# Hi and lo parts of late weights made in the up projection of an encoder layer, and loaded again where they are used

## The chip, the cores and the metric

The kernel runs on one core of one Trainium2 chip. The metric is the device time of one execution in microseconds, the median of several runs.

## The reference

One encoder layer in fp32, with 1024 tokens, width 1024 and a hidden width of 4096. The change touches the last two steps:

```
x = x + (gate_a * y_a + gate_b * y_b) @ w_out            # both attention branches
h = rmsnorm(x, norm_mlp_g)
x = x + square(relu(h @ w_ff1)) @ w_ff2                  # up, then down
gate_p = sigmoid(rmsnorm(x, norm_ple_g) @ w_ple_gate)    # 1024 x 1024
x = x + gate_p * (p @ w_ple)                             # p: 1024 x 256
return rmsnorm(x, final_norm_g)
```

## The kernel before

Every fp32 product is made of three matmuls. An operand is split into a hi part (a copy rounded to float32r, on ScalarE, L235) and a lo part (source minus hi, on VectorE unless another engine is named, L236), and `mm3` (L239) multiplies hi by hi, hi by lo and lo by hi. A matmul is written as 128x512: 128 partitions by 512 columns. Loads and stores go through SyncE's queue (`load`, L232).

Stages in order: input mixing with both attention branches, output mixing with x1 (the residual, also stored to DRAM), the up projection, the down projection, and the per-layer embedding with the final norm. All arrays live in regions of SBUF that open and close: a region that opens over a closed one waits until the old one's readers are done.

**Up (`up`, L1090).** 16 pairs, each 256 columns of `w_ff1`, and each a 2x2 block product by Winograd's scheme, 7 products of 12 matmuls, 84 in all. Per pair SyncE loads w1 into one of two slots (`raw2`), GpSimd makes four sums of its quarters, ScalarE and VectorE split them into the ring `rc` (6 slots of 2048). `relu2` squares the result on ScalarE and stores u (chunks of 128 rows, 32 in all) to DRAM. At the start the normalised input, in four quarters (`hf`), is combined and split into the regions `ha`, `hb` and `hc`.

**Down (`down`, L1150).** 8 blocks of 4 chunks of u and the matching rows of w2. Blocks 0 to 6 are done by Winograd: GpSimd makes the eight sums s and t (L1177 to L1184), both operands are split into `rc`, and each product is added in PSUM order into one of seven accumulators `facc` (VectorE, L1206). Block 7, the plain one, is done directly: its 4 rows of w2 are split (lo on GpSimd), then for each of 8 row tiles u is split, 24 matmuls run, the accumulators are gathered into x1 (44 sums of 128x512, on GpSimd for one column half and VectorE for the other, L1227) and the PSUM result is added (L1252).

**Embedding (`ple`, L1268).** 8 rows of the gate and 2 of the embedding weight are loaded and split (`ple_weights`, `w_rows`). Per row tile, `prepare` loads p, transposes it (L1294), norms and transposes x (L275) and splits both; `finish` runs 48 gate and 12 embedding matmuls, the sigmoid, the product, the final norm and the store.

The order on each engine is set by a scheduler from the program's dependences, unless a stretch is put under `manual_schedule`, which keeps one engine's instructions in the order of the code.

Of the kernel before, what the change touches and what calls it, by code (L numbers as in the profile page):

```python
# [17 lines left out]
P = 128  # L18
S = 1024
# [22 lines left out]
N_GW = 7  # L42

# [182 lines left out]
class Layer:  # L226
# [79 lines left out]
    def run(self):  # L306
# [23 lines left out]
        self.wg, self.rg = [], []  # L330
        self.up()
        self.down()
        self.ple()
# [667 lines left out]
    def mix_outputs(self):  # L1001
# [37 lines left out]
        self.hf = [self.rf[i].take(2048) for i in (0, 1, 1, 0)]  # L1039
# [50 lines left out]
    def up(self):  # L1090
# [15 lines left out]

        def relu2(j, i, u):
            nc.scalar.activation(u, u, AF.Relu)
            nc.scalar.activation(u, u, AF.Square)
            self.load(self.dr["u"][2 * j + i], u)  # L1110
# [35 lines left out]
        wi.run([job(j) for j in range(2, n_pair)], cur)  # L1146
        for region in left[::-1]:
            region.close()

    def down(self):  # L1150
# [66 lines left out]
        for i in range(4):  # L1217
            d = self.wc.next()
            w.append((d[:, :1024], d[:, 1024:]))
            self.split(w[i][0], w[i][1], t[2 + i // 2][:, i % 2, :], g)  # L1220
        us = Ring([d[:, o:o + 1024] for d in (self.wc.next(), self.wc.next()) for o in (0, 1024)])

        def gather(eng, t, c, add, sub=()):
            p = slice(t % 4 * 512, t % 4 * 512 + 512)
            o = x[t][:, 512 * c:512 * c + 512]
            for i in add:
                eng.tensor_tensor(out=o, in0=o, in1=acc[i][:, p], op=ALU.add)  # L1227
            for i in sub:
                eng.tensor_tensor(out=o, in0=o, in1=acc[i][:, p], op=ALU.subtract)

        for r in range(NT):
            self.load(x[r], self.dr["x1"][r * P:(r + 1) * P, :])
        for r in range(NT):
            sl = slice(r * P, (r + 1) * P)
            p = slice(r % 4 * 512, r % 4 * 512 + 512)
            ub = us.next()
            hi, lo = v3(ub[:, :512], 4), v3(ub[:, 512:], 4)
            for i in range(2):
                self.split(hi[:, 2 * i:2 * i + 2, :], lo[:, 2 * i:2 * i + 2, :], t[i][:, :, sl])
# [133 lines left out]
```

## Time and profile before

| what | value |
|---|---|
| median of 3 runs | 1803.49 us (1802.71 to 1805.03) |
| profiled execution, its own time | 1805.11 us |
| its span | 1803.3 us, 22775 instructions |
| TensorE matmul / weight load busy | 1742.9 us (97%) / 1439.7 us (80%) |
| VectorE busy | 1244.7 us (69%) |
| ScalarE busy | 796.4 us (44%) |
| GpSimd busy | 420.5 us (23%) |
| HBM read / written | 146.12 MB / 54.73 MB |

The span runs from the first to the last instruction of one profiled execution, and every time in the rows is counted from its start. In rows PE is TensorE's matmuls, PEld its weight loads (which overlap the matmuls), DVE VectorE, ACT ScalarE, POOL GpSimd and SP SyncE; a q behind an engine's name is its queue of DMA issues. PEclk is the share of full speed that the throttle granted to TensorE. A number in brackets with an arrow is idle time of that engine ahead of the row and what ended it.

### The profile page before, as it was taken

The numbers are of one execution on the slowest core, as the hardware profiler recorded it, in microseconds if no ns is written. First come the engines' busy times: TensorE is split into PE (matmuls) and PEld (weight loads), VectorE is DVE, ScalarE is ACT, GpSimd is POOL, SyncE is SP. The second block draws the span as 40 slices with busy tenths as digits, with TensorE's granted clock in tenths as the row PEclk, the third lists the DMA queues.
The fourth block names the chain that finished last, engine by engine and source line by source line (L and its number), as shares of the span: only waits on it lengthen the run. The fifth ranks groups of instructions, "written<-read, shape, count | busy, mean of one in ns | idle before, by whom it ended". The sixth has DMA issues, their size and how long they took to land.

```text
span 1803.3 us, 22775 instructions
## 1 busy us (share of the span) xinstructions
PE 1742.9 (97%) x8451; PEld 1439.7 (80%) x8451; DVE 1244.7 (69%) x2070; ACT 796.4 (44%) x1383; POOL 420.5 (23%) x234
## 2 busy tenths in 40 slices
PE   6999999999998999999999999999999999989897
PEld 5888888877887888888888778888888888867786
DVE  7556754476765787875455686555569999999564
ACT  6333233266333677774333354443546333332331
POOL 0242322000000000000000134343337666672000
PEclk9999999999999999999999999999999999999999
DMA  6243234475163222225432223333353333331111
GB/s 216 74 154 138 94 117 152 154 230 168 36 180 110 64 42 24 31 24 167 160 129 94 94 82 109 126 105 112 142 207 135 117 116 112 123 128 35 36 38 45
DMA packets 132287, 199.20 MB, mean 110 GB/s; under 512 B 25508, under 2 KB 92932, under 8 KB 132176
## 3 DMA queue, kind: packets, MB, share of 16 engines
q1 hardware_dynamic: 131008, 194.17, 34.0%
q0 software_dynamic: 1168, 3.57, 0.7%
q8 instruction: 67, 1.10, 0.3%
q14 instruction: 44, 0.36, 0.1%
HBM read 146.12 MB, written 54.73 MB: 111 GB/s over the span
## 4 chain that ended last, share of the span: by engine, by line
PE 59%; DVE 7%; issue 1%; ACT 0%; DMA 0%; DVEq 0%; ACTq 0%
PE psum L239 55%; PE psum L936 3%; DVE rc L236 3%; DVE facc L1206 2%; DVE hb L236 0%; PE psum L275 0%; PE psum L1062 0%; DVE fsum L1227 0%; DVE rg L236 0%; ACT fp L930 0%; ACT rc L235 0%; DVE base L926 0%; PE psum L1294 0%; DMA base<-in_p 0%; ACT hb L235 0%
## 5 line engine op out<-in xcount | busy, mean ns | idle before, releaser
L239 PE MATMUL psum<-rc,rc 128*128 128x512 f32 x1464 | 342.2, 394 | 10.4 <-DVE rc L236 9.6
L239 PE MATMUL psum<-rh,rh 128*128 128x512 f32 (+1 forms) x1428 | 335.8, 389 | 1.6 <-ACT rh L235 1.1
L239 PEld LDWEIGHTS psum<-rc,rc 128*128 128x128 f32 x1464 | 277.8, 190 | 71.3 <-DVE rc L236 10.4
L239 PEld LDWEIGHTS psum<-rh,rh 128*128 128x128 f32 x1428 | 260.9, 190 | 59.3 <-issue 5.9
L151 POOL TENSOR_TENSOR base<-base 128x512 f32<-128x512 f32 x17 | 29.0, 1703 | 770.7 <-DMA base<-in_w_ff 604.9
L239 PE MATMUL psum<-ht,rh 128*128 128x512 f32 x624 | 145.7, 389 | 0.0
L239 PE MATMUL psum<-hc,rc 128*128 128x512 f32 x576 | 137.9, 389 | 0.0
L239 PEld LDWEIGHTS psum<-ht,rh 128*128 128x128 f32 x624 | 117.2, 188 | 24.3
L235 ACT ACTIVATE rh<-base 128x512 fp32r<-128x512 f32 (+1 forms) x77 | 61.2, 808 | 147.4 <-PE psum L239 120.2
L239 PEld LDWEIGHTS psum<-hc,rc 128*128 128x128 f32 x576 | 108.1, 188 | 22.4
L236 DVE TENSOR_TENSOR rh<-base,rh 128x512 fp32r<-128x512 f32 (+1 forms) x77 | 78.3, 1027 | 62.8 <-PE psum L239 39.0
L235 ACT ACTIVATE rc<-base 128x1024 fp32r<-128x1024 f32 (+1 forms) x64 | 51.5, 827 | 151.5 <-PE psum L239 147.6
L239 PE MATMUL psum<-ro,rwt 128*128 128x512 f32 x480 | 109.0, 389 | 0.0
L239 PEld LDWEIGHTS psum<-ro,rwt 128*128 128x128 f32 x480 | 90.1, 188 | 18.7
L209 DVE TENSOR_TENSOR fw<-fw,psum 128x512 f32<-128x512 f32 x91 | 74.3, 817 | 42.4 <-PE psum L239 41.4
L239 PE MATMUL psum<-rp,kv 128*128 128x512 f32 x384 | 103.5, 405 | 0.0
L926 DVE TENSOR_REDUCE base<-psum 128x1 f32<-128x1024 f32 x64 | 78.3, 1224 | 36.3 <-PE psum L239 36.3
L239 PE MATMUL psum<-kv,rq 128*128 128x512 f32 x384 | 100.3, 398 | 1.6 <-ACT fp L840 0.9
L1206 DVE TENSOR_TENSOR facc<-facc,psum 128x1024 f32<-128x1024 f32 x84 | 98.5, 1207 | 0.0
L239 PE MATMUL psum<-hb,rc 128*128 128x512 f32 x384 | 93.8, 394 | 4.5 <-DVE hb L236 4.5
L236 DVE TENSOR_TENSOR rc<-fsum,rc 128x1024 fp32r<-128x1024 f32 x56 | 94.2, 1711 | 3.3 <-ACT rc L235 3.3
L236 DVE TENSOR_TENSOR rc<-rfb,rc 128x512 fp32r<-128x512 f32 (+1 forms) x62 | 74.1, 1212 | 31.3 <-ACT rc L235 31.0
(273 smaller groups left out, 3036.2 us busy)
## 6 DMA issues: line engine op xcount, KB each, us to landing
base<-in_w_ff SPq DMA_DIRECT2D x20, 1024.0 KB, 5.5
base<-in_w_in SPq DMA_DIRECT2D x13, 1024.0 KB, 5.3
s_u<-rfa SPq DMA_DIRECT2D x22, 512.0 KB, 2.6
base<-in_w_in SPq DMA_DIRECT2D x20, 512.0 KB, 4.8
fg<-s_gd SPq DMA_DIRECT2D x16, 512.0 KB, 5.8
rfa<-s_u SPq DMA_DIRECT2D x8, 1024.0 KB, 4.9
fraw<-in_w_ff SPq DMA_DIRECT2D x8, 1024.0 KB, 5.8
s_gd<-fw SPq DMA_DIRECT2D x14, 512.0 KB, 3.0
```

The lines of the kernel that those rows point to most:

```text
L151: g.tensor_tensor(out=s1, in0=a21, in1=a22, op=ALU.add)
L209: self.nc.vector.tensor_tensor(out=self.c[out], in0=self.c[a], in1=self.p[i], op=op)
L235: self.nc.scalar.activation(hi, src, AF.Copy)
L236: (eng or self.nc.vector).tensor_tensor(out=lo, in0=src, in1=hi.bitcast(F32), op=ALU.subtract)
L239: self.nc.tensor.matmul(out, lhsT=lhsT, rhs=rhs, start=start, stop=stop)
L926: nc.vector.tensor_reduce(out=nm, in_=ps, axis=AX.X, op=ALU.max, negate=True)
L936: nc.tensor.transpose(pp[:, j * P:(j + 1) * P], probs[j][:, kc * P:(kc + 1) * P], self.ident)
L1206: v.tensor_tensor(out=o, in0=o, in1=ps, op=ALU.add)
```

## The change

The plain block becomes block 1 (chunks 4 to 7), and Winograd takes the other seven, block 7 last. In the up projection a generator `presplit` works through 14 rows of 128 (4 of w2, 8 of the gate, 2 of the embedding), each in two halves: load into the gain slot, split, store hi and lo to new DRAM arrays. `relu2` takes a step or two of it for each chunk of u; chunks 4 to 7 of u are split there as well and stored as hi and lo. After the Winograd blocks, loads on GpSimd's queue bring these parts straight into float32r regions: `rw0` (u hi, over `rfa`), `rw1` (w2 rows 1 and 2, over `rfb`), `rw2` (u lo, over `fraw`), `rw3` (w2 row 0, new space), slots of `rc` (w2 row 3, gate rows 0 to 2), and `rg` over `facc` (gate rows 3 to 7, embedding rows), once all sums are made. All sums run on VectorE. TensorE's order from there to the end is that of the code; a class `Ple` replaces `ple`, norms two row tiles ahead and puts the transposes of the next tile between the two column halves of a tile, those of tile 0 ahead of the last plain row. The matmuls of each product stay the same in number.

```diff
+PLAIN = 1
...
-        self.hf = [self.rf[i].take(2048) for i in (0, 1, 1, 0)]
+        self.hf = [self.rf[i].take(2048) for i in (0, 0, 1, 1)]
...
+        def presplit():
+            spare = self.gain.next()
+            raw, hi = spare[:, :512], spare[:, 512:].bitcast(F32R)
+            w2, wg, wp = io["w_ff2"][0], io["w_ple_gate"][0], io["w_ple"][0]
+            chunks = [("w2s", k, w2[512 * PLAIN + k * P:][:P]) for k in range(4)]
+            chunks += [("wgs", k, wg[k * P:][:P]) for k in range(KD)] + [("wps", k, wp[k * P:][:P]) for k in range(2)]
+            for name, k, src in chunks:
+                for o in (0, 512):
+                    self.load(raw, src[:, o:o + 512])
+                    self.split(hi, raw.bitcast(F32R), raw)
+                    yield
+                    for i, a in enumerate((hi.bitcast(F32), raw)):
+                        self.load(self.dr[name][k, i, :, o:o + 512], a)
+                    yield
...
         def relu2(j, i, u):
             nc.scalar.activation(u, u, AF.Relu)
             nc.scalar.activation(u, u, AF.Square)
-            self.load(self.dr["u"][2 * j + i], u)
+            c = 2 * j + i
+            if c // 4 != PLAIN:
+                self.load(self.dr["u"][c], u)
+                if c and c != 4 * PLAIN + 4:
+                    next(pre, None)
+                next(pre, None)
+                return
+            if c % 4 == 0:
+                next(pre, None)
+            hi = self.gain.next()
+            self.split(hi.bitcast(F32R), u.bitcast(F32R), u)
+            for n, a in enumerate((hi, u)):
+                self.load(self.dr["us"][c % 4, n], a)
...
+        for _ in pre:
+            pass
...
-        fs, fa, fr = (Region(tc, n, F32, "left") for n in ("fsum", "facc", "fraw"))
-        self.fs = fs
...
-        raw = Ring([self.raw2.slots[0], self.hf[2], self.raw2.slots[1], self.hf[1], self.hf[0], self.hf[3]]
+        raw = Ring([self.raw2.slots[0], self.hf[2], self.hf[3], self.raw2.slots[1], self.hf[1], self.hf[0]]
                    + [fr.take(2048) for _ in range(2)])
...
-        for b in range(nb - 1):
-            for i, pa, pb in plan(b, fetch(b)):
-                product(i, pa, pb, b == 0)
...
-        t = fetch(nb - 1)
-        self.rf[1].close()
-        self.ple_weights(0)
-        w = []
...
+        for n, b in enumerate([b for b in range(nb) if b != PLAIN]):
+            for i, pa, pb in plan(n, fetch(b)):
+                product(i, pa, pb, n == 0)
...
+        def fetch_hl(home, src):
+            for i, a in enumerate(halves(home)):
+                nc.gpsimd.dma_start(a, src[i])
+            return halves(home)
+        def fetch_u(home, n, i):
+            nc.gpsimd.dma_start(v3(home, 2), self.dr["us"][2 * n:2 * n + 2, i].rearrange("c p t -> p c t"))
+            return v3(home, 2)
...
+        for region in (fr, *self.rf[::-1]):
+            region.close()
+        rw = [Region(tc, f"rw{i}", F32R, "right") for i in range(4)]
+        homes = [[r.take(2048) for _ in range(n)] for r, n in zip(rw, (2, 2, 2, 1))]
+        pa = rw[1].ring(2, 512)
+        wc = [self.wc.slots[(self.wc.i + 2 + i) % 6] for i in range(6)]
+        w2s, wgs = self.dr["w2s"], self.dr["wgs"]
+        u = [[fetch_u(home, n, i) for n, home in enumerate(homes)] for i, homes in enumerate((homes[0], homes[2]))]
+        w = [fetch_hl(homes[3][0], w2s[0])]
+        fetch_x(0, 4, 1, 5)
+        w.append(fetch_hl(homes[1][0], w2s[1]))
+        fetch_x(3)
+        w.append(fetch_hl(homes[1][1], w2s[2]))
+        fetch_x(2, 6)
+        w.append(fetch_hl(wc[0], w2s[3]))
+        gp = self.gain.next()
+        self.gain_row(gp, io["norm_ple_g"][0])
+        wg = [fetch_hl(wc[1], wgs[0])]
+        fetch_x(7)
+        wg += [fetch_hl(wc[2 + i], wgs[1 + i]) for i in range(2)]
...
+        def sums(r):
...
                 v.tensor_tensor(out=acc[5][:, p], in0=acc[5][:, p], in1=acc[0][:, p], op=ALU.add)
-                gather(g, r, 0, (0, 1))
-                gather(v, r, 1, (5, 4, 2))
...
+                gather(r, 1, (5, 4, 2))
             else:
-                g.tensor_tensor(out=acc[6][:, p], in0=acc[6][:, p], in1=acc[5][:, p], op=ALU.add)
-                gather(g, r, 0, (6,), (3,))
-                gather(v, r, 1, (6, 4))
+                v.tensor_tensor(out=acc[6][:, p], in0=acc[6][:, p], in1=acc[5][:, p], op=ALU.add)
+                gather(r, 0, (6,), (3,))
...
+        def row(r):
+            sl = slice(r * P, (r + 1) * P)
             ps = ps_r.next()
             for i in range(4):
-                self.mm3([ps[:, 0:512], ps[:, 512:1024]], (hi[:, i, :], lo[:, i, :]),
+                n, k = divmod(i, 2)
+                self.mm3([ps[:, 0:512], ps[:, 512:1024]], (u[0][n][:, k, sl], u[1][n][:, k, sl]),
...
-        fr.close()
-        fa.close()
...
-    def ple_weights(self, part):
-        rg = Region(self.tc, f"rg{part}", F32R, ("right", "left")[part])
-        for k in (range(3), range(3, KD))[part]:
...
-        def prepare(t):
...
+        ple = Ple(self, gp, wg, wc[4:], pa, [self.raw.slots[i] for i in (0, 1, 2)], self.raw.slots[3])
+        with tc.manual_schedule(engines={mybir.EngineType.PE}):
+            for r in range(4):
+                sums(r)
+                row(r)
+                sums(r + 4)
+            fa.close()
+            rg = Region(tc, "rg", F32R, "left")
+            rg_ = [rg.take(2048) for _ in range(7)]
+            for r in range(4, NT):
+                if r == 4:
+                    wg += [fetch_hl(rg_[i], wgs[3 + i]) for i in range(5)]
+                    ple.wp = [fetch_hl(rg_[5 + i], self.dr["wps"][i]) for i in range(2)]
+                row(r)
+                if r == 4:
+                    ple.scale(0)
+                elif r == 6:
+                    ple.turn_p(0)
+                    ple.turn_x(0)
+                    ple.scale(1)
+            rw[3].close()
+            rw[2].close()
+            fy = Region(tc, "fy", F32, "right")
+            ple.run(fy.ring(6, 1024))
...
+    def scale(self, t):
...
+        l.load(pr, l.io["p"][0, 0, t * P:(t + 1) * P, :])
+        r = l.row_rstd(x, xs)
+        nc.vector.scalar_tensor_tensor(xs, x, r, self.gain, op0=ALU.mult, op1=ALU.mult)
...
+            if c == 0 and t + 1 < NT:
+                self.turn_p(t + 1)
+                self.turn_x(t + 1)
+            if c == 1 and t + 2 < NT:
+                self.scale(t + 2)
```

Three places show the order of the program before and now.

TensorE, where the last Winograd product ends (`psum1` is a PSUM buffer; operands are the right-hand rows, then the left-hand tile). Before:

```order
L239 MATMUL psum1_85<-rc4_6950,rc3_6949 128x512 x24
L239 MATMUL psum1_85<-rc6_6952,rc5_6951 128x512 x24
L239 MATMUL psum1_85<-rc1_6947,rc5_6951 128x512 x6
L239 MATMUL psum1_85<-rc2_6948,rc5_6951 128x512 x6
L239 MATMUL psum1_85<-rc3_6949,rc5_6951 128x512 x6
L239 MATMUL psum1_85<-rc4_6950,rc5_6951 128x512 x6
```

The same place after:

```order
L240 MATMUL psum1_85<-rc4_6950,rc3_6949 128x512 x24
L240 MATMUL psum1_85<-rc6_6952,rc5_6951 128x512 x24
L240 MATMUL psum1_85<-rw31_11248,rw01_11242 128x512 x4
L240 MATMUL psum1_85<-rw31_11248,rw21_11246 128x512 x2
L240 MATMUL psum1_85<-rw11_11244,rw01_11242 128x512 x4
L240 MATMUL psum1_85<-rw11_11244,rw21_11246 128x512 x2
```

Row 0 took w2 rows from four `rc` slots and u from a fifth, all of them split on chip; it now takes both from the loaded regions (the two groups behind these: `rw12` and `rc3` with `rw02` and `rw22`). Hi and lo parts of u stand in different regions, so each group of six reads as four and two.

GpSimd, from the last Winograd block's preparation on (`fsum` are the sums s and t of a block, `facc` the product accumulators). Before:

```order
L1181 TENSOR_TENSOR fsum4_9507<-rfb2_6955,fsum2_9505 128x1024
L1182 TENSOR_TENSOR fsum3_9506<-base14_75 128x1024
L1183 TENSOR_TENSOR fsum7_9510<-rfb1_6954,base14_75 128x1024
L1184 TENSOR_TENSOR fsum8_9511<-fsum6_9509,rfb1_6954 128x1024
L1227 TENSOR_TENSOR fsum1_9504<-fsum1_9504,facc1_9512 128x512
L1227 TENSOR_TENSOR fsum1_9504<-fsum1_9504,facc2_9513 128x512
```

After:

```order
L1211 TENSOR_TENSOR fsum4_9659<-rfb1_6955,fsum2_9657 128x1024
L1252 DMA rw21_11246<-s_us 128x2x1024
L1252 DMA rw22_11247<-s_us 128x2x1024
L1212 TENSOR_TENSOR fsum3_9658<-base14_75 128x1024
L1213 TENSOR_TENSOR fsum7_9662<-base14_75,rfb2_6956 128x1024
L1252 DMA rw01_11242<-s_us 128x2x1024
L1214 TENSOR_TENSOR fsum8_9663<-fsum6_9661,base14_75 128x1024
L1252 DMA rw02_11243<-s_us 128x2x1024
L1248 DMA rw11_11244<-s_w2s 128x1024 x2
L1248 DMA rw12_11245<-s_w2s 128x1024 x2
L1248 DMA rc3_6949<-s_w2s 128x1024 x2
L1248 DMA rc4_6950<-s_wgs 128x1024 x2
```

GpSimd's sums (L1227) are gone. Three of the four loads of u now stand between or ahead of its last sums of the block, and the loads of w2 and of the gate behind them. (The names `fsum4` and so on are one tile each; the last Winograd block was block 6 before and is block 7 now.)

VectorE at the start of the up projection (`hb`, `hc` hold the split quarters of the normalised input, `base15` is the gain slot). Before:

```order
L1124 TENSOR_TENSOR rfa1_6953<-rfb1_6954,rfa1_6953 128x2048
L236 TENSOR_TENSOR hb2_7622<-rfa2_6956,hb1_7621 128x2048
L236 TENSOR_TENSOR hb4_7624<-rfa1_6953,hb3_7623 128x2048
L1129 TENSOR_TENSOR rfa2_6956<-rfa2_6956,rfa1_6953 128x2048
L236 TENSOR_TENSOR hc4_7631<-rfb1_6954,hc3_7630 128x2048
```

After:

```order
L1153 TENSOR_TENSOR rfa1_6953<-rfa2_6954,rfa1_6953 128x2048
L237 TENSOR_TENSOR hb2_7622<-rfb2_6956,hb1_7621 128x2048
L237 TENSOR_TENSOR base15_76<-base15_76 128x512
L237 TENSOR_TENSOR hb4_7624<-rfa1_6953,hb3_7623 128x2048
L1158 TENSOR_TENSOR rfb2_6956<-rfb2_6956,rfa1_6953 128x2048
L237 TENSOR_TENSOR hc4_7631<-rfa2_6954,hc3_7630 128x2048
```

The split of the first weight piece (`base15`) now stands between the two splits that fill `hb`; the rest of the sequence is the same, with two quarters in each other's region.

## Rows read from the trace of the kernel before

**Rows 1.** Busy by stretches: us, engines' busy us, granted clock, DMA share, GB/s

```profile
1100.00:1200.00 100.00, 100.00 (x443) 82.84 (x442) 54.83 (x69) 42.41 (x56) 35.88 (x21) 1.00 0.31 106
1500.00:1600.00 100.00, 99.62 (x438) 81.69 (x438) 99.97 (x74) 35.38 (x36) 68.17 (x24) 1.00 0.36 122
1600.00:1700.00 100.00, 84.77 (x358) 67.96 (x357) 85.32 (x154) 32.20 (x53) 30.30 (x16) 0.90 0.15 49
```

**Rows 2.** TensorE in order of time: start, us, instruction, [idle before <-releaser]

```profile
1574.77 35.34 PE L239 MATMUL psum<-rc,rc 128*128 128x512 f32 x155
1615.89 4.70 PE L239 MATMUL psum<-rc,rc 128*128 128x512 f32 x12 [5.78 <-DVE rc L236]
1624.37 42.60 PE L239 MATMUL psum<-rc,rc 128*128 128x512 f32 x176 [3.77 <-DVE rc L236]
1668.38 0.63 PE L275 MATMUL psum<-base,fy 128*128 128x128 f32 x4 [1.42 <-DVE fsum L1252]
1672.81 0.66 PE L1294 MATMUL psum<-base,base 128*128 128x128 f32 x2 [3.79 <-DMA base<-in_p]
```

**Rows 3.** Busy time of a 10-us stretch at the waits

```profile
1610.00:1620.00 10.00, 4.22 (x12) 3.13 (x12) 10.00 (x8) 0.67 (x2) 10.00 (x6) 0.66 0.17 65
```

**Rows 4.** Two pairs of the up projection in order of time, several engines

```profile
1182.12 0.38 SPq L232 DMA_DIRECT2D base<-in_w_ff  x1
...
1187.80 2.10 POOL L151 TENSOR_TENSOR rfb<-base 128x512 f32<-128x512 f32 x1 [11.81 <-DMA base<-in_w_ff]
1188.71 5.60 PE L239 MATMUL psum<-ha,rc 128*128 128x512 f32 x24
...
1193.19 0.69 DVE L236 TENSOR_TENSOR rc<-rfb,rc 128x512 fp32r<-128x512 f32 x1 [1.04 <-ACT rc L235]
...
1205.00 1.06 ACT L235 ACTIVATE rc<-base 128x1024 fp32r<-128x1024 f32 x1 [4.81 <-PE psum L239]
1207.75 5.60 PE L239 MATMUL psum<-ha,rc 128*128 128x512 f32 x24
```

**Rows 5.** The chain that ended last, in the embedding: start, us, engine, what

```profile
1705.96 0.22 PE psum L1294 x2
...
1765.19 0.22 PE psum L1294 x2
1767.03 26.57 PE psum L239 x117
```

**Rows 6.** VectorE in order of time, last splits, sums and a row add

```profile
1598.95 1.21 DVE L236 TENSOR_TENSOR rc<-rfb,rc 128x1024 fp32r<-128x1024 f32 x1
...
1612.09 2.35 DVE L1227 TENSOR_TENSOR fsum<-fsum,facc 128x512 f32<-128x512 f32 x2
...
1644.24 1.28 DVE L1227 TENSOR_TENSOR fsum<-fsum,facc 128x512 f32<-128x512 f32 x2
1645.44 1.21 DVE L1252 TENSOR_TENSOR fsum<-fsum,psum 128x1024 f32<-128x1024 f32 x1
```

**Rows 7.** GpSimd in order of time, the last sum of the last Winograd block

```profile
1564.22 2.42 POOL L1184 TENSOR_TENSOR fsum<-fsum,rfb 128x1024 f32<-128x1024 f32 x1 [1.22 <-DVE rc L236]
```

**Rows 8.** GpSimd's own loads, line L616: issue ns min/median/max, then landing

```profile
L616 POOL DMA_DIRECT2D s_vec<-s_row x12: 523/526/569, 83.4 to 96.8; - x12
...
DMA to landing us min/median/max: 3.6/5.1/7.2
```

**Rows 9.** DMA queues, 78 to 105 us: packets, MB, share of 16 engines

```profile
q0 software_dynamic: 1056, 3.17, 38.5%
```

**Rows 10.** Busy time of two stretches with many loads

```profile
95.00:100.00 5.00, 5.00 (x35) 4.63 (x34) 2.54 (x5) 2.23 (x4) 2.07 (x4) 1.00 0.61 152
1570.00:1574.00 4.00, 4.00 (x19) 3.32 (x18) 4.00 (x4) 2.01 (x2) 0.00 (x0) 1.00 0.83 289
```

**Rows 11.** Start of the up projection in order of time

```profile
1037.47 8.62 DVE L236 TENSOR_TENSOR hb<-rfa,hb 128x2048 fp32r<-128x2048 f32 x2 [0.50 <-ACT hb L235]
1046.14 6.73 PE L239 MATMUL psum<-hb,rc 128*128 128x512 f32 x22 [4.48 <-DVE hb L236]
```

More of the change, by code (lines that the diff above doesn't have):

```diff
@@ L329, in run @@
         self.mix_outputs()
-        self.wg, self.rg = [], []
         self.up()
         self.down()
-        self.ple()
         pad.close()
@@ L1105, in up @@
         s_hf, s_own = tiles[6:], [self.g_ring.slots[0], self.rs]
+        def presplit():
[12 more added lines that the diff above has]
+                    yield
+        pre = presplit()
         def relu2(j, i, u):
@@ L1153, in down @@
         v, g = nc.vector, nc.gpsimd
-        fs, fa, fr = (Region(tc, n, F32, "left") for n in ("fsum", "facc", "fraw"))
-        self.fs = fs
+        fs, fa, fr = (Region(tc, n, F32, s) for n, s in (("fsum", "left"), ("facc", "left"), ("fraw", "right")))
         st = [fs.take(1024) for _ in range(8)]
         acc = [fa.take(2048) for _ in range(7)]
-        raw = Ring([self.raw2.slots[0], self.hf[2], self.raw2.slots[1], self.hf[1], self.hf[0], self.hf[3]]
+        raw = Ring([self.raw2.slots[0], self.hf[2], self.hf[3], self.raw2.slots[1], self.hf[1], self.hf[0]]
                    + [fr.take(2048) for _ in range(2)])
@@ L1206, in product, with halves, fetch_x, gather @@
                     v.tensor_tensor(out=o, in0=o, in1=ps, op=ALU.add)
-        for b in range(nb - 1):
-            for i, pa, pb in plan(b, fetch(b)):
-                product(i, pa, pb, b == 0)
-        t = fetch(nb - 1)
-        self.rf[1].close()
-        self.ple_weights(0)
-        w = []
[L1217 to L1223, printed above, removed]
+        for n, b in enumerate([b for b in range(nb) if b != PLAIN]):
+            for i, pa, pb in plan(n, fetch(b)):
+                product(i, pa, pb, n == 0)
+        def halves(home):
+            return home[:, :1024], home[:, 1024:]
+        def fetch_hl(home, src):
[5 more added lines that the diff above has]
+            return v3(home, 2)
+        def fetch_x(*rows):
+            for r in rows:
+                self.load(x[r], self.dr["x1"][r * P:(r + 1) * P, :])
+        for region in (fr, *self.rf[::-1]):
[18 more added lines that the diff above has]
+        wg += [fetch_hl(wc[2 + i], wgs[1 + i]) for i in range(2)]
+        def gather(t, c, add, sub=()):
             p = slice(t % 4 * 512, t % 4 * 512 + 512)
@@ L1226, in gather @@
             for i in add:
-                eng.tensor_tensor(out=o, in0=o, in1=acc[i][:, p], op=ALU.add)
+                v.tensor_tensor(out=o, in0=o, in1=acc[i][:, p], op=ALU.add)
             for i in sub:
[L1229 to L1234, printed above, removed]
+                v.tensor_tensor(out=o, in0=o, in1=acc[i][:, p], op=ALU.subtract)
@@ L1235, in down @@
+        def sums(r):
             p = slice(r % 4 * 512, r % 4 * 512 + 512)
[L1236 to L1239, printed above, removed]
             if r < 4:
                 v.tensor_tensor(out=acc[5][:, p], in0=acc[5][:, p], in1=acc[0][:, p], op=ALU.add)
-                gather(g, r, 0, (0, 1))
-                gather(v, r, 1, (5, 4, 2))
-            else:
-                g.tensor_tensor(out=acc[6][:, p], in0=acc[6][:, p], in1=acc[5][:, p], op=ALU.add)
-                gather(g, r, 0, (6,), (3,))
-                gather(v, r, 1, (6, 4))
+                gather(r, 0, (0, 1))
+                gather(r, 1, (5, 4, 2))
+            else:
+                v.tensor_tensor(out=acc[6][:, p], in0=acc[6][:, p], in1=acc[5][:, p], op=ALU.add)
+                gather(r, 0, (6,), (3,))
+                gather(r, 1, (6, 4))
@@ L1351, in build @@
                         ("ub", (3, 2, P, S)), ("nd", (3, S, 2 * HG)), ("wd", (3, HG, S)), ("ob", (2, P, S)), ("gd", (16, P, S)), ("qd", (HA, P, S)),
-                        ("rd", (2 * HA, 4, P)), ("x1", (S, D)), ("u", (FF // P, P, S))):
+                        ("rd", (2 * HA, 4, P)), ("x1", (S, D)), ("u", (FF // P, P, S)),
+                        ("us", (4, 2, P, S)), ("w2s", (4, 2, P, D)), ("wgs", (KD, 2, P, D)), ("wps", (2, 2, P, D))):
         scratch[name] = nc.dram_tensor("s_" + name, shape, F32, kind="Internal").ap()
```

126 lines of the change are left out of this document (58 added, 68 removed).

## The prediction

> **What bounds the kernel now.** I read the busy time by stretches first. TensorE is busy 97% of the span, so only the stretches below that can give anything. From 1100 to 1200 us it is busy throughout at a granted clock of 1.00; 1500 to 1600 is nearly full too, although VectorE is at 99.97 of 100 there. What is left in the part that the change touches is 1600 to 1700, with 84.77 us and a clock of 0.90 [rows 1]. Then TensorE in order of time: the last Winograd product ends at 1574.77 + 35.34 = 1610.11, then come 5.78 us idle, 12 matmuls, 3.77 us idle, and the rest of the plain block until 1666.97. Both waits end with VectorE's splits (L236). Behind them stand 1.42 us for the norm and 3.79 us for a load of `p` [rows 2]. In the 10-us stretches around these waits the granted clock is 0.66, between the two levels 1.2 and 2.4 GHz, so the matmuls beside the waits run slowly too [rows 3].
>
> The loss is the time taken minus the dense price. Dense: a pair of the up projection, 84 matmuls of 512 columns, takes 1207.75 - 1188.71 = 19.04 us [rows 4], 0.2267 us each. The plain block has 192 (8 rows x 4 chunks x 6), 43.5 us dense; it took 1666.97 - 1610.11 = 56.9 us: 13.4 lost. The embedding (60 matmuls and 10 transposes per row tile) runs steadily at (1765.19 - 1705.96)/4 = 14.81 us per tile [rows 5], 118.5 for 8; it took from 1666.97 to 1793.60, that is 126.6: 8.1 lost. Together **21.5 us**. The 9.7 us behind the last matmul (to 1803.3) belong to the last tile's own chain, which the change leaves as it is.
>
> **The change part by part.**
>
> *Removed at the end.* ACT and VectorE no longer split the plain block's u (16 lo splits), its w2 (4, on POOL), the gate's 8 and the embedding's 2 weight rows. TensorE then needs only what loads bring: its stream goes from the last product straight into `rw`/`rc` operands, and the first tile's transposes stand before row 7, so the norm and the `p` load have rows to hide behind. Matmul counts stay. If nothing else is late, the 21.5 us go, and the clock loss with them.
>
> *VectorE at the end.* It takes over POOL's sums: 44 of 128x512 at 0.60 (two take 1644.24 to 1645.44 with POOL empty, [rows 6]) = 26.6 us, and 8 row adds of 1.21 = 9.7 (L1252, [rows 6]). That is 36.3 us against 43.5 us of rows, part of it already between the last products. Walking its new order from 1577.85 with these prices, the last split of the a22 quarter comes at about 1597.3 (1598.95 before), row 0's add at 1616.6 (TensorE frees it at 1615.5), the last sum at about 1632.5. Each row needs the PSUM slot of four rows earlier, 16 us of cover. Cost 0; between -1 (TensorE's crumbs at 1500 to 1600 are 0.4 us) and, if each sum took 1.18 us, as the two at 1612.09 with POOL beside them, 25.5 more, less the 7.2 that the rows leave and some 3 between the products: +15.
>
> *POOL at the end.* Its last tensor instruction is the t4 of the last Winograd block, at 1564.22 [rows 7]; behind it only loads queue, 0.53 us of issue each [rows 8], and nobody on POOL waits behind them. The three loads of u that stand ahead of t4 wait for the last splits of the block before, as t4 does; t4 is split behind the a22 quarter, 34 us later. The waits that matter are two. First, `rw1` (w2 rows 1 and 2) opens after the a22 split, 1597.3; the third (rc3) after the second-last product, 1604.7. TensorE wants row 0's four chunks at 1610.1, 1611.5, 1612.8 and 1614.2. Second, `rg` (5 gate rows, 2 embedding rows, 7.34 MB) opens when the last sum has read the accumulators, 1632.5; TensorE wants its last row at 1660.8 (1610.1 + 43.5 of rows + 1.1 of transposes + 24 gate matmuls, 5.4, + 3 of the embedding, 0.7).
>
> The price of these loads is the unknown: no row shows a load into a float32r tile. The nearest is the POOL queue itself, in its only busy stretch: 3.17 MB in 38.5% of 27 us, 305 GB/s of full occupancy [rows 9], a 256-KB load landing in 3.6 us at the least [rows 8], so 2.7 us of latency. Ends: 348 GB/s (0.83 busy, 289 GB/s) and 152 GB/s, what moved while four of POOL's loads were out [rows 10]. At 305, w2 rows 1 to 3 (3.15 MB) and three x1 rows (1.57 MB) from 1600.0 need 15.5 us: 1615.5, **1.3 us late**. `rg` from 1633.8 + 2.7 needs 24.1: 1660.6, against 1660.8 + 1.3 = 1662.1: in time. At 348 neither is late. At 152 the first ends at 1631.2 (17 late), the next three gate rows at 1651.9, `rg` at 1700.2, 22.4 late more.
>
> The Trainium skill (DMA: Bandwidth & Descriptors, section "Measured") states 341 GB/s for 1 MB issued from GpSimd; by it `rg` would take an estimated 21.5 us and neither would be late. The same page says that a float32r destination always makes the load a cast (section "SWDGE vs HWDGE vs iDMA"), for which it gives no rate, and no run here shows one.
>
> *Up projection.* Added: 28 pieces (14 rows in halves), each a 256-KB load, an ACT and a VectorE split, two 256-KB stores, and 4 splits of u. VectorE: 28 x 0.69 [rows 4] + 4 x 1.21 = 24.2 us over 16 pairs, 304 us, where it is busy 55% [rows 1]. SP's queue now has stores that wait for a split ahead of the next w1 load. That load issues at 1182.12, POOL starts on it at 1187.80, and ACT splits it at 1205.00 only, when a product frees the ring [rows 4]: 17 us of cover, and TensorE uses it a pair later still. One piece is, as an estimate from these rows, 3.6 to load, 0.7 and 0.7 to split, 3.6 to store, 8.6 us; two, 17.2, fit a pair of 19.04. Cost 0.
>
> At the start of this stage there is no cover: TensorE waits 4.48 us for hb, whose two lo splits took 8.62 us because POOL ran beside them [rows 11]. One piece's split of 0.69 now stands between the two. Its load is issued once the norm's gain row is read, ahead of this stage, and lands before ACT reaches it. **+0.7**, between 0 (if it fits the contended stretch) and 2.
>
> *Moved.* Block 1 becomes the plain one and Winograd takes block 7 last: same counts; other homes in the ring; the u of the last pair is now needed six blocks later. Cost 0.
>
> Sum: -21.5 + 0.7 + 1.3 = **-19.5 us**. The profiled execution took 1805.11 us (span 1803.3), giving 1785.6; the median of the runs shown is 1803.49, 1.6 below it, so **1784.0**.
>
> **Rivals.**
>
> *A, the loads are partly late.* At 220 GB/s w2 ends at 1621.5 (7.3 late) and `rg` at about 1632.5 + 7.3 + 2.7 + 33.4 = 1675.9 against 1668.1 (7.8 late): 1782.7 + 15 = 1798. For it: the 152 GB/s stretch. Against: the queue was not kept full in it. Typical for this case: 1793.
>
> *B, the other side: the casting loads run well below plain ones.* From 1600.0 to the last embedding row 15.2 MB must land (4.72 + 3.15 + 7.34). Without a loss that is until 1660.8; the whole gain of 20.8 is gone at 1681.6, 81.6 us, 186 GB/s. Below it the kernel is slower: at 152, 1782.7 + 39.4 = 1822, and the clock would fall in the waits again. Against: POOL's own 305.
>
> The Trainium skill (SBUF — State Buffer, box "The DVE blocks DMA trap") says that loads issued from GpSimd stall in descriptor generation while VectorE runs an operation in a two-port mode. That would be a road to B. No operation of the new tail but the small tensor_scalars is of that kind, and the trace's POOL issues took 523 to 569 ns; its stretch had VectorE mostly idle, so it doesn't settle it.
>
> *C, the pieces hold up the up projection.* If a piece took 11 us, 14 pairs lag 3 us each, 42 us, against 36 of cover (17 and a pair): with the stall at the ends about 10 us, 1794. Against: ACT is 42% busy there and each piece has a gap of its own behind the s4 split.
>
> *D, VectorE is late with the sums*, since they now stand ahead of Winograd adds that free PSUM: half of the +15 above, 1791. Against: POOL, which doubled VectorE's prices, is empty there.
>
> **How the numbers follow.** Forecast 0.60, A 0.14, B 0.10, C 0.07, D 0.09. The forecast alone: 1781 (nothing late, 1782.7, and a us of crumbs) to 1789. The range takes in A and most of C and D: 1780 to 1800. About 0.2% (3.6 us) is what a measurement of this kernel can tell from no change. Faster than 1799.9: forecast, D, C and most of A: 0.86. Within 0.2%: the slow end of A and the fast end of B: 0.05. Slower: 0.09.
>
> **What would show it.** Right: no wait of TensorE over 2 us from the last product to the last matmul, granted clock 1.00 in every 10-us stretch there, the plain rows in 43 to 46 us; POOL without tensor work behind t4; the hb wait at 5.2 us; full up pairs at 19.04. Wrong: a TensorE wait released by a load into rw, rc or rg (A, B), by VectorE with the sums (D), or up pairs longer than 19.1 us (C). If the loads from `s_wgs` run below 186 GB/s with their queue full, the forecast fails altogether.

## The result, and the profile after

The changed kernel took **1784.71 us** (median of 4 runs, 1784.23 to 1786.01) against 1803.1 in the runs of before beside it: ratio 0.9898, interval 0.9883 to 0.9912. The forecast was 1784.0, in a range from 1780 to 1800. The profiled execution took 1784.23, with a span of 1782.5.

TensorE in order of time from the last Winograd product on, columns as in [rows 2]:

```profile
1569.75 38.92 PE L240 MATMUL psum<-rc,rc 128*128 128x512 f32 x171
1608.51 4.24 PE L240 MATMUL psum<-rw,rw 128*128 128x512 f32 x18
1612.59 1.52 PE L240 MATMUL psum<-rc,rw 128*128 128x512 f32 x6
...
1646.59 0.38 PE L1360 MATMUL psum<-base,base 128*128 128x128 f32 x2
1648.07 1.09 PE L1370 MATMUL psum<-base,base 128*128 128x128 f32 x8 [1.09 <-DVE fsum L1306]
1648.91 4.37 PE L240 MATMUL psum<-rw,rw 128*128 128x512 f32 x18
1653.12 1.52 PE L240 MATMUL psum<-rc,rw 128*128 128x512 f32 x6
1656.21 2.32 PE L240 MATMUL psum<-rc,rc 128*128 128x512 f32 x9 [1.57 <-issue]
...
1771.75 1.52 PE L240 MATMUL psum<-rg,rw 128*128 128x512 f32 x6
```

The waits of 5.78, 3.77, 1.42 and 3.79 us are gone. Two are left: 1.09 us for a row add (L1306, a row's PSUM result added into x1), and 1.57 us that the profile puts down to nothing it shows. It ends with the add of row 7, at 1656.1:

```profile
1646.79 1.22 DVE L1306 TENSOR_TENSOR fsum<-fsum,psum 128x1024 f32<-128x1024 f32 x1 [4.22 <-PE psum L240]
...
1654.90 1.21 DVE L1306 TENSOR_TENSOR fsum<-fsum,psum 128x1024 f32<-128x1024 f32 x1
```

The stretch from 1600 to 1700, and three shorter ones with the loads (columns as in [rows 1]):

```profile
1600.00:1700.00 100.00, 97.33 (x449) 80.51 (x448) 76.45 (x191) 20.10 (x38) 11.67 (x22) 1.00 0.44 156
...
1604.00:1608.00 4.00, 4.00 (x19) 3.34 (x18) 4.00 (x7) 0.00 (x0) 1.50 (x3) 1.00 1.12 398
1608.00:1616.00 8.00, 8.00 (x37) 6.60 (x37) 8.00 (x13) 0.00 (x0) 2.12 (x4) 1.00 1.12 404
...
1640.00:1648.00 8.00, 6.97 (x32) 5.53 (x30) 3.09 (x4) 0.38 (x1) 2.64 (x5) 1.00 1.15 415
```

TensorE is busy 97.33 us in place of 84.77, at a granted clock of 1.00 in place of 0.90. In the three short stretches, full of loads into float32r, 398 to 415 GB/s moved. GpSimd in order of time:

```profile
1563.75 2.40 POOL L1214 TENSOR_TENSOR fsum<-fsum,base 128x1024 f32<-128x1024 f32 x1 [0.55 <-DVE rc L237]
...
1597.51 2.16 POOL L1248 DMA_DIRECT2D rw<-s_w2s  x4 [30.66 <-issue]
1603.31 1.13 POOL L1248 DMA_DIRECT2D rc<-s_w2s  x2 [3.65 <-PE psum L240]
...
1632.77 3.71 POOL L1248 DMA_DIRECT2D rg<-s_wgs  x7 [21.70 <-DVE fsum L1284]
...
1645.51 0.53 POOL L1248 DMA_DIRECT2D rg<-s_wps  x1 [0.75 <-issue]
```

`rw1` opens at 1597.5 (forecast 1597.3), `rc` at 1603.3 (1604.7), `rg` at 1632.8 (1632.5). At the start of the up projection the first piece stands between the two splits of `hb`:

```profile
1035.09 6.67 POOL L1156 TENSOR_TENSOR rfa<-rfb,rfa 128x2048 f32<-128x2048 f32 x1 [8.96 <-ACT hb L236]
...
1035.08 2.29 DVE L237 TENSOR_TENSOR hb<-rfb,hb 128x2048 fp32r<-128x2048 f32 x1
1037.29 5.02 DVE L237 TENSOR_TENSOR base<-base 128x512 fp32r<-128x512 f32 x1
1042.23 2.28 DVE L237 TENSOR_TENSOR hb<-rfa,hb 128x2048 fp32r<-128x2048 f32 x1
...
1044.57 7.51 PE L240 MATMUL psum<-hb,rc 128*128 128x512 f32 x22 [5.77 <-DVE hb L237]
```

The piece took 5.02 us there, with a GpSimd sum beside it; the two splits with the piece between take 9.4 us, where [rows 11] has 8.62 without it. (In the run *again*, below, the split ahead of the piece took 6.39 us beside that sum, and the piece 0.68; the three together took 9.2.)

### The profile page after: what moved, and what is told of

Its sections match the earlier page's. It is cut to its first block, busy times and chain, and to the rows that moved or that the text cites. A ratio compares the mean times of both kernels' runs of the same rounds, so it can differ in the third digit from the quotient of the medians.

```text
span 1782.5 us, 22922 instructions
## 1 busy us (share of the span) xinstructions
PE 1734.3 (97%) x8451; PEld 1434.9 (80%) x8451; DVE 1255.6 (70%) x2096; ACT 794.7 (45%) x1385; POOL 391.1 (22%) x242
## 4 chain that ended last, share of the span: by engine, by line
PE 65%; DVE 1%; issue 1%; ACT 0%; DVEq 0%; ACTq 0%
PE psum L240 61%; PE psum L935 3%; DVE rc L237 0%; PE psum L1370 0%; PE psum L1061 0%; ACT fp L929 0%; DVE base L925 0%; DVE hb L237 0%; ACT hb L236 0%; PE psum L1360 0%; DVE fx L1055 0%; DVE fsum L1306 0%; DVE fx L1077 0%; PE psum L834 0%; ACT rc L236 0%
## 5 line engine op out<-in xcount | busy, mean ns | idle before, releaser
L240 PE MATMUL psum<-rc,rc 128*128 128x512 f32 x1320 | 304.2, 390 | 2.0 <-issue 1.6
L240 PEld LDWEIGHTS psum<-rc,rc 128*128 128x128 f32 x1320 | 246.7, 188 | 55.2 <-issue 4.2
L240 PEld LDWEIGHTS psum<-ro,rwt 128*128 128x128 f32 x480 | 90.1, 188 | 18.7
L236 ACT ACTIVATE rc<-fsum 128x1024 fp32r<-128x1024 f32 x56 | 57.4, 1055 | 85.3 <-issue 65.9
L240 PE MATMUL psum<-ha,rc 128*128 128x512 f32 x384 | 91.4, 394 | 0.0
```

Source lines behind the costliest of these rows:

```text
L236: self.nc.scalar.activation(hi, src, AF.Copy)
L240: self.nc.tensor.matmul(out, lhsT=lhsT, rhs=rhs, start=start, stop=stop)
```

## The experiments

Totals move by 2 us and more between executions of one program, so each profile is cut in stretches; they repeat far better. All in us. *Start*: first `ha` matmul to first `hc` matmul. *Down*: first matmul of the down projection to the last Winograd product's end. *Tail*: from there to the end of the last matmul. From the first `hc` matmul to the down projection it was 288.32 or 288.33 in every run. Each ratio is to runs of the kernel before beside that run.

| run | start | down | tail | median of 4 | ratio to before (interval) |
|---|---|---|---|---|---|
| before | 30.16 | 269.08 | 183.47 | 1803.1 | 1 |
| changed | 30.91 | 268.28 | 164.76 | 1784.71 | 0.9898 (0.9883 to 0.9912) |
| again | 31.96 | 269.13 | 164.77 | 1786.09 | 0.9900 (0.9886 to 0.9915) |
| plain_raw | 32.15 | 272.50 | 171.82 | 1795.04 | 0.9944 (0.9925 to 0.9963) |
| gate_raw | 30.93 | 268.63 | 172.82 | 1792.75 | 0.9934 (0.9918 to 0.9951) |
| gate_raw_psum | 32.17 | 268.51 | 163.36 | 1784.68 | 0.9894 (0.9880 to 0.9909) |
| loads_twice | 30.99 | 268.99 | 194.19 | 1816.34 | 1.0061 (1.0046 to 1.0076) |
| sums_pool | 32.09 | 270.99 | 171.10 | 1792.72 | 0.9939 (0.9924 to 0.9954) |
| late_turn | 30.61 | 270.78 | 165.29 | 1788.26 | 0.9914 (0.9897 to 0.9930) |
| late_piece | 30.65 | 272.52 | 164.75 | 1788.34 | 0.9911 (0.9895 to 0.9928) |
| psum | 32.04 | 270.00 | 161.65 | 1783.74 | 0.9883 (0.9868 to 0.9898) |
| psum2 | 32.07 | 272.14 | 161.63 | 1784.19 | 0.9885 (0.9865 to 0.9904) |
| wp_raw_psum | 31.99 | 268.29 | 161.65 | 1782.56 | 0.9875 (0.9861 to 0.9890) |
| best | 31.98 | 268.34 | 163.16 | 1782.00 | 0.9872 (0.9855 to 0.9888) |

The run *again* is the changed kernel unedited:

> The changed kernel once more, unedited, as the measure for the runs beside it. All theories: 1783 to 1787, ratio to before 0.988 to 0.991. Its two waits of 1.09 and 1.57 us at the end of the plain rows come again.

Both waits came again, 1.10 and 1.58 us. My theory was that the early parts bring the gain because TensorE no longer waits for splits on the chip; the main rival, that TensorE's new order brings it.

**The plain block's parts, made late (plain_raw).**

```diff
+        def fetch_raw(home, src):
+            hi, lo = halves(home)
+            nc.gpsimd.dma_start(lo, src)
+            self.split(hi, lo, lo.bitcast(F32))
+            return hi, lo
...
-        w = [fetch_hl(homes[3][0], w2s[0])]
+        w = [fetch_raw(homes[3][0], w2r[0])]
```

The other rows of w2 and the chunks of u are loaded in the same way, and the up projection makes no parts of them.

> Leaves out the early parts of the plain block alone: its four chunks of u and four rows of w2 are loaded once, rounded to float32r by the load (so their lo parts come out as zero), into the same homes, on the same queue, and split there on ScalarE and VectorE. The order of TensorE, the sums and all weights of the embedding stay as in the changed kernel. My theory (the gain is the on-chip splits that TensorE waited for): eight more lo splits of 128x1024, 8 x 1.21 = 9.7 us, on a VectorE that is 99.97 of 100 us busy up to the plain block; TensorE waits 5 to 10 us for VectorE at row 0 and its first groups, time 1789 to 1795. Rival, order (the gain comes from TensorE's hand-set order, the transposes ahead and the two-tile lead): no more than 1 us is lost, 1784 to 1786.

Tail 171.82, 7.1 more than changed. ScalarE, VectorE and TensorE at the wait of the tail:

```profile
1616.71 1.07 ACT L236 ACTIVATE rc<-rc 128x1024 fp32r<-128x1024 f32 x1 [2.27 <-DMA rc<-in_w_ff]
...
1622.71 1.22 DVE L237 TENSOR_TENSOR rc<-rc 128x1024 fp32r<-128x1024 f32 x1
...
1623.98 2.08 PE L240 MATMUL psum<-rc,rw 128*128 128x512 f32 x4 [4.24 <-DVE rc L237]
```

As the theory had it, TensorE stands for a split, that of the fourth w2 row (rc): 4.24 us, a little under the 5 to 10 expected; the other 2.8 fit the granted clock, 0.97 from 1600 to 1700. The split could have run at 1617.8, when ScalarE's copy was done, and stood for 4.9 us behind sums and adds in VectorE's queue. The down projection lost 4.2 more, in waits of 0.5 and 0.9 us; VectorE splits w2 row 0 in its first block, at 1354.6, but that this is the cause isn't shown.

**The gate and embedding parts, made late (gate_raw),** the same edit on the ten other rows.

> Leaves out the early parts of the gate and embedding weights alone: the ten rows are loaded once, rounded by the load (lo parts come out as zero), into the same homes on the same queue, and split there. My theory: VectorE is idle for 23.5 of the 100 us from 1600 to 1700 and the first of these rows is wanted at 1656; 10 x 1.21 = 12.1 us of lo splits and 10 copies on ScalarE fit, and the loads are half the bytes: 1784 to 1788, no TensorE wait of over 2 us released by a split. Rival, the ten rows' early parts bring the 8.1 us that the embedding lost: 1790 to 1793, with TensorE waiting for splits of rg. Rival, order: 1784 to 1785.

A miss: tail 172.82, 8.1 more, the rival's size, though by another way. VectorE, then TensorE, then the clock of a 10-us stretch:

```profile
1645.20 1.22 DVE L237 TENSOR_TENSOR rg<-rg 128x1024 fp32r<-128x1024 f32 x1 [1.08 <-ACT rg L236]
1646.34 1.21 DVE L1313 TENSOR_TENSOR fsum<-fsum,psum 128x1024 f32<-128x1024 f32 x1
1647.47 2.35 DVE L237 TENSOR_TENSOR rg<-rg 128x1024 fp32r<-128x1024 f32 x2
1649.74 1.21 DVE L1313 TENSOR_TENSOR fsum<-fsum,psum 128x1024 f32<-128x1024 f32 x1
```

```profile
1651.01 1.97 PE L1377 MATMUL psum<-base,base 128*128 128x128 f32 x8 [5.17 <-DVE fsum L1313]
1653.62 6.79 PE L240 MATMUL psum<-rw,rw 128*128 128x512 f32 x18 [0.63 <-DVE rw L237]
...
1663.17 2.30 PE L240 MATMUL psum<-rc,rc 128*128 128x512 f32 x9 [1.40 <-DVE fsum L1313]
```

```profile
1650.00:1660.00 10.00, 8.35 (x25) 6.64 (x26) 9.10 (x20) 2.34 (x4) 0.00 (x0) 0.56 0.00 0
```

Row 6's add was ready when its matmuls ended (1645.6). It ran at 1649.7, behind splits that had waited for their loads, and the transposes of tile 0 waited for it. Then TensorE ran at 0.56, near the lower level: its next 18 matmuls took 6.79 us instead of 4.37. VectorE had the time for the splits, but the row add had lost its place in the queue.

**The PSUM banks (psum, and once more as psum2).** Why do the transposes wait for a row's add? Winograd products and rows take four PSUM slots of two banks each in turn. 98 half products come before the rows, so row 6 uses banks 0 and 1, where the transposes go, and row 7 banks 2 and 3, where the first gate sum goes.

```diff
-        self.ps_t, self.ps_g, self.ps_p = Ring(layer.bank2[:1]), Ring(layer.bank[2:6]), Ring(layer.bank[6:])
+        self.ps_t, self.ps_g, self.ps_p = Ring(layer.bank2[2:3]), Ring(layer.bank[6:] + layer.bank[2:4]), Ring(layer.bank[:2])
```

> The row tiles' PSUM banks of the embedding are dealt anew: transposes into banks 4 and 5 (plain row 4), gate sums in 6, 7, 2, 3, embedding sums in 0 and 1. Two waits are left in the changed kernel's tail: 1.09 us for row 6's add ahead of the transposes of tile 0 and 1.57 us for row 7's add ahead of the first gate matmul. My theory: both are PSUM banks that the rows still hold (row 6 in banks 0 and 1, row 7 in 2 and 3), so both go: -2.6 us, 1782.1. Rival: the 1.57 us wait is for the last loads of rg or for the split of the normed tile, and stays: 1783.6 or 1784.7.

> The changed kernel with the PSUM banks dealt anew (as psum), once more, as the measure beside the next run. Theory: its tail is 2.7 to 3.1 us shorter than the changed kernel's, 1782 to 1784; in some executions 2.2 to 2.9 us are lost in the first 45 us of the down projection (waits for facc and rc splits near 1350 to 1383), where the last pieces' stores stand in SyncE's queue ahead of the first w2 loads.

Both waits went, so the 1.57 us too was the add of row 7; the tail is 161.65 and 161.63, 3.1 less. TensorE is full in the stretch that had 84.77 us before the change:

```profile
1600.00:1700.00 100.00, 100.00 (x462) 83.19 (x461) 79.61 (x195) 20.12 (x38) 13.88 (x26) 1.00 0.45 158
```

By the ratios the total is 2 to 3 us lower, within the intervals. The spans of the two profiles (1782.4 and 1786.3) don't show it, since these executions lost 1.7 and 3.9 us early in the down projection (below); for the same reason psum's median, 1783.74, lies at the rival's 1783.6, though its trace speaks against the rival.

**Late gate parts with free banks (gate_raw_psum).**

> Late splits of the ten gate and embedding rows (as in gate_raw: loaded once, rounded, lo parts zero) together with the PSUM banks dealt anew (as in psum). In gate_raw TensorE stood 5.17 us ahead of the transposes of tile 0, for row 6's add, which VectorE had ready to run at 1645.5 but reached at 1649.7 behind splits that waited for their loads; then the granted clock fell to 0.56. My theory, mended: what the early parts of the gate save is not VectorE's time but its queue. With the transposes in a bank that no late row holds, that wait goes; what stays is the split of the normed tile behind the last splits of rg (1654 in gate_raw, where row 7 would now end at 1652): a wait of 1 to 4 us and some clock, 1784 to 1788. Rival (the splits cost VectorE's time itself, 8 us): 1790 to 1792.

Tail 163.36: only 1.7 more than psum, one wait of 1.37 us for a row add, and not for the split of the normed tile that was expected. So the ten rows' early parts are worth 8.1 us with the changed kernel's banks and 1.7 with others: what they save is mostly that row add's place. This also limits my theory: with the plain block's parts early, the new order and free banks, the embedding keeps all but 1.7 us of its gain even with late splits of its own weights.

**The order alone (late_turn),** `turn_p(0)` and `turn_x(0)` moved behind row 7.

> The transposes of tile 0 and of its p stand behind plain row 7 in TensorE's order, as they did before the change, in place of ahead of it. My theory (the hand-set order is worth little by itself): TensorE waits for ScalarE's copy (1.02) and VectorE's lo split (1.23) of the transposed tile, 2 to 3.5 us and some clock, but the 1.09 us wait ahead of the transposes goes and the 1.57 us is covered: 0 to 2 us more, 1785 to 1787. Rival, order (the 8.1 us that the embedding lost before are the transposes behind the last row): 1790 to 1793.

Tail 165.29, 0.5 more. With early parts in place the rival (8 us for these transposes) falls; the median, 1788.26, lies above the 1785 to 1787 expected, and the profile shows 2.5 us more in the down projection (270.78). The rest of the new order, the norms two tiles ahead above all, was not taken back in any run.

**Sums on GpSimd again (sums_pool),** column half 0 of `gather`, and the adds into accumulator 6.

> The accumulators' sums for column half 0, and the adds of accumulator 5 into 6, go back to GpSimd as before; all else as in the changed kernel. GpSimd's queue then has 8 sums ahead of the w2 loads, and the rg loads wait for its last one. My theory: the loads are issued in program order behind sums, w2 rows 1 and 2 at about 1598 to 1601 and row 3 at 1606 to 1608, near their limit of 1612.6; sums of 1.18 us on VectorE with GpSimd beside it: 24 x 0.58 = 14 us more on VectorE in place of 20 x 0.60 = 12 us less; rg opens 0 to 8 us later. 1785 to 1792, any wait of TensorE at a load of rw, rc or rg. Rival (it makes no difference who does the sums): 1784 to 1785.

Tail 171.10, 6.3 more; the median, 1792.72, is just above the range expected. GpSimd and TensorE:

```profile
1599.05 3.43 POOL L1285 TENSOR_TENSOR fsum<-fsum,facc 128x512 f32<-128x512 f32 x2 [2.37 <-DMA fsum<-s_x]
1603.90 2.19 POOL L1248 DMA_DIRECT2D rw<-s_w2s  x4 [1.43 <-DVE rc L237]
1610.01 3.51 POOL L1296 TENSOR_TENSOR facc<-facc,facc 128x512 f32<-128x512 f32 x2 [3.92 <-DVE facc L1236]
...
1615.17 1.12 POOL L1248 DMA_DIRECT2D rc<-s_w2s  x2
```

```profile
1619.23 0.73 PE L240 MATMUL psum<-rc,rw 128*128 128x512 f32 x2 [3.69 <-DMA rc<-s_w2s]
```

The fourth w2 row (rc) is loaded from 1615.2 instead of 1603.3, behind sums that wait for accumulators. TensorE's new waits end with that load, none with VectorE: that the sums left GpSimd matters because its queue carries the loads.

**Loads issued twice (loads_twice).**

> Every load of a w2, gate or embedding part is issued twice into the same place, 23 MB in place of 11.5. My theory (timely loads are what TensorE's stream rests on, at the 400 to 415 GB/s that the changed kernel's trace shows): the last w2 row lands at 1597.5 + 2.7 + 6.3 MB / 405 GB/s = 1615.8 where TensorE wants it at 1612.6, 3 late; the rg rows take 1632.8 + 3 + 2.7 + 14.7 MB / 405 GB/s = 1675 where the last is wanted at about 1662 + 3, 10 late: 1794 to 1801, with TensorE's waits released by loads. If the loads had slack of a factor of two, as a rival would have it that takes the gain from the order alone: 1785 to 1787.

Slower than before, and by more than expected:

```profile
1617.95 2.07 PE L240 MATMUL psum<-rw,rw 128*128 128x512 f32 x4 [5.62 <-DMA rw<-s_w2s]
...
1678.52 1.22 PE L240 MATMUL psum<-rg,rc 128*128 128x512 f32 x2 [5.88 <-DMA rg<-s_wgs]
...
1687.49 0.79 PE L240 MATMUL psum<-rg,rw 128*128 128x512 f32 x1 [4.35 <-DMA rg<-s_wps]
```

```profile
1654.31 0.54 POOL L1249 DMA_DIRECT2D rg<-s_wgs  x1 [6.34 <-DMA rg<-s_wgs]
```

```profile
1612.00:1620.00 8.00, 2.38 (x7) 1.52 (x6) 6.01 (x10) 0.00 (x0) 3.20 (x6) 0.66 0.96 308
```

I had counted 405 GB/s. But a second copy waits until the first has landed, and what stands behind it in GpSimd's queue waits too, 6.34 us in the first line; in stretches of 8 and 10 us from 1604 to 1680 292 to 331 GB/s moved, half of it of use. That is 146 to 166 GB/s, where the prediction's rival B gave 1822 (at 152); 1816 was measured.

**The first piece (late_piece),** its data read from the stored u chunk 0.

> The changed kernel, but the first piece (half of w2 row 0) reads its data from the stored first chunk of u, so that row's parts are wrong and its split comes after the splits of hb and hc. Theory: the first piece's split between the two of hb is the whole of the loss at the start of the up projection; TensorE's wait there falls from 5.2 to 6.2 us to about 4.5, and the stretch from the first ha matmuls to the first hc matmuls returns from 30.9 to 30.2 us. All else as the changed kernel: 1784 to 1786. Rival (the wait belongs to the swapped homes of the quarters): it stays.

```profile
1042.97 7.72 PE L240 MATMUL psum<-hb,rc 128*128 128x512 f32 x22 [5.26 <-DVE hb L237]
```

The wait was 5.26 us, not 4.5; the start took 30.65, between before (30.16) and the others, which fall in two groups, 30.6 to 31.0 and 31.9 to 32.2, with the piece in place in both. The date at which `hb` is ready, counted from the first `ha` matmul, is steadier. It is 23.57 us in changed, gate_raw and loads_twice, whose eight transposes (L1061) ahead of it took 1.09 us, and 23.09 here, with 1.17; where the transposes took 1.97, it is 24.13 to 24.17 with the piece and 23.59 before. So the piece delays `hb` by some 0.5 us. The rest of the start is TensorE's speed: plain_raw and late_turn both have `hb` at 24.14 and both waited 6.15 us, but the 22 matmuls behind the wait took 8.18 and 6.63 us, at a granted clock of 0.58 and 0.72 over the 12 us there, and their starts are 32.15 and 30.61. Why the clock differs isn't shown.

**The late pieces (wp_raw_psum, best).** In five of eight profiles with all 28 pieces and w2's parts made early, TensorE loses 1.7 to 4.2 us in the first 45 us of the down projection. SyncE, VectorE and TensorE of psum2:

```profile
1313.73 1.13 SPq L234 DMA_DIRECT2D s_wps<-base  x2
1318.60 0.38 SPq L234 DMA_DIRECT2D rfb<-in_w_ff  x1
```

```profile
1344.64 1.21 DVE L1215 TENSOR_TENSOR fsum<-fsum,base 128x1024 f32<-128x1024 f32 x1
```

```profile
1356.85 22.29 PE L241 MATMUL psum<-rc,rc 128*128 128x512 f32 x97 [0.97 <-ACT facc L1235]
...
1386.21 185.07 PE L241 MATMUL psum<-rc,rc 128*128 128x512 f32 x815 [0.96 <-DVE rc L238]
```

VectorE of changed, which doesn't have the loss, and SyncE of best:

```profile
1335.25 2.83 DVE L1214 TENSOR_TENSOR fsum<-fsum,base 128x1024 f32<-128x1024 f32 x1
```

```profile
1310.95 0.38 SPq L233 DMA_DIRECT2D rfb<-in_w_ff  x1
```

That load of w2 is issued 24.7 us ahead of the first down matmul (1343.32) in psum2, behind the stores of a piece. Over the eight it is 28.7 to 28.9 in the three without the loss and 22.7 to 27.8 in the five with it; in gate_raw, gate_raw_psum and wp_raw_psum, whose pieces end earlier, 30.2 each time, without the loss. (plain_raw, with 30.3, also lost time there, see above.) What the load feeds shows how it costs: in the first block VectorE, not GpSimd, makes the four sums t from w2 (L1208 to L1214, in psum2 one line lower). In the seven profiles without the loss its last one ends 2.15 us ahead of the first down matmul; in the five it ends 1.0 (psum), 1.9 (late_turn and sums_pool), 2.5 (psum2) and 3.1 us (late_piece) behind it, and they lose 1.7, 2.5 and 2.7, 3.9 and 4.2 us, in the same order. In wp_raw_psum the two embedding rows are loaded once and split late; best does so in full precision, from a slot that is free:

```diff
-                    ple.wp = [fetch_hl(rg_[5 + i], self.dr["wps"][i]) for i in range(2)]
+                    ple.wp = []
+                    for i in range(2):
+                        stage, home = self.g_ring.slots[0], halves(rg_[5 + i])
+                        self.load(stage, io["w_ple"][0][i * P:(i + 1) * P, :])
+                        self.split(*home, stage)
+                        ple.wp.append(home)
```

> PSUM banks dealt anew, and the two embedding rows no longer made early: they are loaded once (rounded by the load, lo parts zero) into their place in rg, last in the queue, and split there by ScalarE and VectorE. The up projection then works 24 pieces in place of 28, done some two pairs (38 us) before its end. Theory: the loss at the start of the down projection is the last pieces' traffic in SyncE's queue, so it goes (no wait over 0.5 us from 1340 to 1390), and the two late splits (2.4 us) fit behind row 7's first half: 1781 to 1783.5. Rival (that loss is a matter of the execution and not of the pieces): it shows here as often, and the time equals psum2's within 1 us.

> The PSUM banks dealt anew, and the two embedding rows left out of the early pieces in full precision: each is loaded as fp32 into the slot that later holds the last gain row, and split from there into its place in rg as soon as the sums have freed it. 24 pieces in the up projection in place of 28. Theory: as wp_raw_psum, a tail of 161.65 us from the first plain matmul to the last one, no wait over 0.5 us in the first 50 us of the down projection, its first w2 load into rfb issued 30.2 us ahead of the first down matmul as in the runs without late pieces; 1781 to 1783.5, ratio to before 0.986 to 0.989. Rival (the start of the down projection is a matter of the execution): that load is issued under 28.9 us ahead, and 2 to 4 us are lost there.

In both that loss went. best has one wait of 0.95 us there all the same (with the load 31.3 us ahead), whose cause isn't shown, and 1.37 us for a row add behind a split, so its tail is 163.16 and not the 161.65 expected. That the pieces' stores cause the loss fits these profiles but rests on few: three of the eight with all pieces escaped it too, and the kernel before, in another order, has its last t 1.2 us behind the first down matmul without such waits. best has the lowest median, 1782.00, and leaves nothing out; its interval overlaps those of psum2 and of the changed kernel, so that it beats the latter is likely, not shown. It beats the kernel before.

## Why the prediction was right

**The loss and its price.** Forecast: 21.5 us of waits and slow clock in the tail, dense 162.0. psum shows the dense tail: 161.65. The changed kernel's is 164.76, so it took 18.7 of 21.5. How the 18.7 divide isn't settled: taking the early parts of the plain block away costs 7.1, those of the gate 8.1 or, with free banks, 1.7, the sums back on GpSimd 6.3; these don't add, and no run takes away both kinds of parts. That late splits cost TensorE waits is shown; that they are the whole of the gain is not.

**The sum.** Between the two profiles the span fell by 20.8: tail 18.71, behind the last matmul 0.49, down projection 0.80, and 1.55 ahead of the first `ha` matmul, where that matmul comes at 1019.5 to 1022.9 in all runs; less 0.75 at the start of up. Forecast was 19.5. That the median lies 0.7 from the forecast is partly luck: two terms of the tail were off with opposite signs (1.3 that didn't come, 2.66 missed), and the 2.84 us gained outside the tail, more than the tail fell short, lie in stretches that have no gain in the prediction's sum and that move as much between runs.

**The 1.3 us for late w2 rows** didn't come. I took 305 GB/s from [rows 9]; 398 to 415 were measured. The Trainium skill's 341 GB/s, stated for a transfer of 1 MB (DMA: Bandwidth & Descriptors, section "Measured"), is nearer, and low too for this queue of loads. VectorE was busy 4.00 of 4 us with sums, adds and splits while 398 GB/s moved, so a stall of the loads isn't seen with them. The descriptor stall that the Trainium skill (SBUF — State Buffer, box "The DVE blocks DMA trap") states is for operations in a two-port mode, which these stretches don't test.

**The 2.66 us of PSUM waits** I missed. I counted the slot of four rows earlier for the rows, but not which banks the embedding's first tiles take over.

**VectorE and GpSimd at the end.** Costs 0, as forecast; the three dates came within 1.4 us. But the reason why GpSimd must be empty is its queue of loads (sums_pool), more than the price of VectorE's sums, on which rival D rested.

**The up projection.** Its pairs cost nothing (288.32), against rival C. At its start +0.7 was forecast: the stretch grew by 0.75 in this profile and by 1.8 in again, of which the piece is some 0.5 (late_piece). At its end the pieces do cost, as far as shown: 1.7 to 4.2 us in some executions, a small form of C that I had excluded, since I counted cover against w1's loads only and not against the down projection's first.

**Rivals A and B** failed on the rate; loads_twice shows that at some 150 GB/s of use the kernel would indeed have been slower than before. The Winograd order's move cost nothing that shows.

## What to carry to other kernels

Making operands early, in a stage with idle engines, pays when the late stage waits for splits; a late split costs by its place in its engine's queue, by what stands ahead of it (plain_raw) and behind it (gate_raw), and in both runs more than by its own time. Where one stage hands PSUM over to the next, work out which bank the last user holds. And work that is slipped into a stage must be counted against the loads of the next stage too, if they share a queue.

## What the runs showed that I had not expected

- With loads of 512 KB from GpSimd's queue into float32r 398 to 415 GB/s moved, at a DMA share of 1.12 to 1.15. After seven in a row, GpSimd issued the others 1.24 to 2.23 us apart.
- A split of 128x512 took 5.02 us beside a GpSimd sum of 128x2048, 0.68 in again behind that sum; which of VectorE's splits meets the sum changes between executions.
- The tail of one program repeats within 0.02 us between executions (164.75 to 164.77 in the three profiles whose tail has the same code), while its total moves by 2 us and more: stretches tell edits apart that totals can't.
